# A hybrid retention and SSD layer rewritten with a lifetime-bound list scheduler, prompts first

## The chip, the cores and the metric

The kernel runs on the 8 cores of one Trainium2 chip, each core with its own part of the batch. The metric is the device time of the slowest core, in microseconds (us). A program on all eight cores has a second, slower state in some executions, in which one die, or both, has a lower granted clock. The ratios below use fast runs alone; a median is that of all runs listed, and where one of them was slow the text says so.

Engine names: PE is the matrix engine (PEld its weight loads), DVE the vector engine, ACT the activation engine, POOL the GpSimd engine, SP the engine that issues part of the DMAs. PSUM is the memory, in banks, that PE writes its products to; SBUF holds the other data on the core (one block, `arena`, in these traces). A slab is a block of weights fetched by one DMA, a ring a set of buffers used in turn. A list scheduler takes the ready operations one by one, by priority, and so fixes each engine's order before the program runs.

## The reference, cut to what matters

One layer of a backbone with two head groups. Every core gets one sample (1,024 tokens) and two prompts (256 tokens each): 1,536 tokens of width 1,024. Data lie in memory as fp32, matrix products are taken in bf16.

```python
def rms_norm(x):                      # per token and head, over 128 features
    return x * lax.rsqrt(jnp.mean(jnp.square(x), axis=-1, keepdims=True) + EPS)

def trunk_layer(x, mod, rope, s_ret0, s_ssd0, p):
    sh1, sc1, g1, sh2, sc2, g2 = jnp.split(mod, 6, axis=-1)     # from silu(cond) @ w_ada
    h = x * (1 + sc1) + sh1
    q, k, v, g, z, xbc, dt_raw = jnp.split(h @ p['w_in'], IN_SPLITS, axis=-1)
    # A: bidirectional retention, 4 heads of 128
    o_ret, sr_f, sr_b = bidir_scan(q, k, v, v, lg_f, lg_b, ...)
    o_ret = jax.nn.silu(g) * rms_norm(o_ret)                    # <- the wide rsqrt
    # B: bidirectional Mamba-2 SSD, 8 heads (conv, scan, gated norm) -> o_ssd
    mix = jnp.concatenate([o_ret, o_ssd], axis=-1) @ p['w_out']
    x = layer_norm(ALPHA * x + g1 * mix, ...)
    h2 = x * (1 + sc2) + sh2
    ffn = (jax.nn.silu(h2 @ p['w_gate']) * (h2 @ p['w_up'])) @ p['w_down']   # d_ff 2816
    return layer_norm(ALPHA * x + g2 * ffn, ...), states
```

## The kernel before

The program before records its operations, orders each engine's queue by a list scheduler with fixed buffers, and runs the stages one after the other: modulation, all projections (sample and prompts together), retention, conv and SSD, output projection, FFN. Retention works in units of one head and 512 sample tokens or 256 prompt tokens, 16 units in all. Features lie on the partitions there, so the norm's `rsqrt` is needed for a whole tile, 128 partitions by 512 or 256 columns, not for one number per token. It is taken on ACT as `exp(-0.5*ln(x))`:

```python
def rstd_from(dst, src_ps_or_sb, scale, reads, writes):
    act(dst, src_ps_or_sb, AF.Ln, ..., bias=epsb[:, 0:1], scale=scale)
    act(dst, dst, AF.Exp, writes, writes, scale=-0.5)

def ret_unit(t0, nb, h, r0, W):              # W = 512 (sample) or 256 (prompt)
    ...                                      # cut: scores, decay mask, weighted sum of v into PS(ob)
    act(sqb_[:, 0:W], PS(ob, W), AF.Square, [pk(ob)], [skey])
    mm(PS(msb, W), ones_b[:], sqb_[:, 0:W], True, True, ...)       # sum of squares over partitions
    rstd_from(rsf_[:, 0:W], PS(msb, W), 1.0 / 128.0, [pk(msb)], [rkey])
    tt(rsf_[:, 0:W], PS(ob, W), rsf_[:, 0:W], ALU.mult, ...)
    tt(oT[:, h, ...], rsf_[:, 0:W], gT[:, h, ...], ALU.mult, ..., eng=POOL)
```

Of the kernel before, what the change touches and what calls it, by code (L numbers as in the profile page):

```python
# [8 lines left out]
BF16 = mybir.dt.bfloat16  # L9
U8 = mybir.dt.uint8  # L10
AF = mybir.ActivationFunctionType
ALU = mybir.AluOpType
SZ = {F32: 4, BF16: 2}

PE, ACT, DVE, POOL, SP = "tensor", "scalar", "vector", "gpsimd", "sync"
ENGS = [PE, ACT, DVE, POOL, SP]

D = 1024
NT = 1536
NTT = 12  # L20
INC = 3592
DFF = 2816
EPS = 1e-6
ALPHA = 2.0 ** 0.25
NEG = -32768.0
SEQS = [(0, 8), (8, 2), (10, 2)]

class Op:
    __slots__ = ("idx", "eng", "fn", "is_dma", "dsem", "dval", "deps", "inc", "cval", "cost", "fin", "npend", "succ", "start", "crit", "tag", "aps")

    def __init__(self, idx, eng, fn, is_dma):
        self.idx, self.eng, self.fn, self.is_dma = idx, eng, fn, is_dma
        self.dsem, self.dval, self.deps, self.inc, self.cval = None, 0, [], False, 0
        self.cost, self.fin, self.npend, self.succ = 0.3, 0.0, 0, []
        self.start, self.crit, self.tag, self.aps = 0.0, None, '', None

class Prog:
    def __init__(self, nc):
        self.nc = nc
        self.ops = []  # L40
        self.res = {}
        self.dma_sems = {}
        self.out_dma_ops = []
        self.cur_tag = ""
        self.last_dma = {}

    @staticmethod
    def _split(key):
        if isinstance(key, tuple):
            return key[0], tuple(key[1:])  # L50
        return key, ()

    @staticmethod
    def _related(p, q):
        n = min(len(p), len(q))
        return p[:n] == q[:n]

    def _record(self, op, reads, writes):
        deps = set()
        for k in reads:  # L60
            name, p = self._split(k)
            d = self.res.setdefault(name, {})
            for q, e in d.items():
                if self._related(p, q) and e[0] is not None:
                    deps.add(e[0])
        for k in writes:
            name, p = self._split(k)
            d = self.res.setdefault(name, {})
            for q, e in d.items():
                if self._related(p, q):  # L70
                    if e[0] is not None:
                        deps.add(e[0])
                    deps.update(e[1])
        deps.discard(op)
        op.deps = sorted(deps, key=lambda o: o.idx)
        for k in reads:
            name, p = self._split(k)
            d = self.res[name]
            if p not in d:
                d[p] = [None, []]  # L80
            d[p][1].append(op)
        for k in writes:
            name, p = self._split(k)
            d = self.res[name]
            for q in [q for q in d if len(q) >= len(p) and q[:len(p)] == p]:
                del d[q]
            d[p] = [op, []]

    def op(self, eng, fn, reads=(), writes=(), cost=0.3):
        o = Op(len(self.ops), eng, fn, False)  # L90
        o.cost = cost
        o.tag = self.cur_tag
        self.ops.append(o)
        self._record(o, list(reads), list(writes))
        return o

    def dma(self, eng, fn, semkey, reads=(), writes=(), is_output=False, cost=3.0, chain=True):
        o = Op(len(self.ops), eng, fn, True)
        o.cost = cost
        o.tag = self.cur_tag  # L100
        ent = self.dma_sems.setdefault(semkey, [None, 0])
        ent[1] += 16
        o.dsem, o.dval = semkey, ent[1]
        self.ops.append(o)
        self._record(o, list(reads), list(writes))
        prev = self.last_dma.get(semkey)
        if chain and prev is not None and prev not in o.deps:
            o.deps.append(prev)
            o.deps.sort(key=lambda q: q.idx)
        self.last_dma[semkey] = o  # L110
        if is_output:
            self.out_dma_ops.append(o)
        return o

    def schedule(self):
        import heapq
        ops = self.ops
        for o in ops:
            o.succ = []
        for o in ops:  # L120
            o.npend = len(o.deps)
            for d in o.deps:
                d.succ.append(o)

        def lat(d, o):
            return 0.05 if (d.eng == PE and o.eng == PE and not d.is_dma and not o.is_dma) else 0.25

        bl = [0.0] * len(ops)
        for o in reversed(ops):
            m = 0.0  # L130
            for s_ in o.succ:
                v = bl[s_.idx] + lat(o, s_)
                if v > m:
                    m = v
            bl[o.idx] = o.cost + m
        inorder = {SP: False, POOL: False, PE: False, ACT: False, DVE: False}
# [3 lines left out]
        ready_t = {}  # L140
        nxt = {e: 0 for e in ENGS}
        eng_ops = {e: [o for o in ops if o.eng == e] for e in ENGS}
        order = {e: [] for e in ENGS}

        def push(o):
            rt = 0.0
            for d in o.deps:
                rt = max(rt, d.fin + lat(d, o))
            ready_t[o.idx] = rt
            heapq.heappush(pend[o.eng], (rt, o.idx, o))  # L150

        for o in ops:
            if o.npend == 0:
                push(o)
        done, n = 0, len(ops)
        while done < n:
            best = None
            for e in ENGS:
                if inorder[e]:
                    if nxt[e] >= len(eng_ops[e]):  # L160
                        continue
                    o = eng_ops[e][nxt[e]]
                    if o.npend != 0 or o.idx not in ready_t:
                        continue
                    st_ = max(tcur[e], ready_t[o.idx])
                    cand = (st_, o.idx, e, o)
                else:
                    p, a = pend[e], avail[e]
                    while p and p[0][0] <= tcur[e]:
                        rt, idx, o = heapq.heappop(p)  # L170
                        heapq.heappush(a, (-bl[idx], idx, o))
                    if a:
                        o = a[0][2]
                        cand = (tcur[e], o.idx, e, o)
                    elif p:
                        rt, idx, o = p[0]
                        cand = (rt, idx, e, o)
                    else:
                        continue
                if best is None or cand[:2] < best[:2]:  # L180
                    best = cand
            assert best is not None, "scheduler deadlock"
            st_, _, e, o = best
            if inorder[e]:
                nxt[e] += 1
            else:
                if avail[e] and avail[e][0][2] is o:
                    heapq.heappop(avail[e])
                else:
                    heapq.heappop(pend[e])  # L190
            o.start = st_
            o.crit = ("eng", order[e][-1]) if (order[e] and tcur[e] >= ready_t[o.idx]) else \
                ("dep", max(o.deps, key=lambda d: d.fin) if o.deps else None)
            if o.is_dma:
                tcur[e] = st_ + (1.0 if e == POOL else 0.1)
                o.fin = st_ + o.cost
            else:
                tcur[e] = st_ + o.cost
                o.fin = tcur[e]
            order[e].append(o)  # L200
            done += 1
            for s_ in o.succ:
                s_.npend -= 1
                if s_.npend == 0:
                    push(s_)
# [3 lines left out]
    def emit(self, stack, reorder=True):  # L209
        nc = self.nc  # L210
        if reorder:
            order = self.schedule()
        else:
            order = {e: [o for o in self.ops if o.eng == e] for e in ENGS}
        esem = {e: stack.enter_context(nc.semaphore("c_" + e)) for e in ENGS}
        for i, (k, ent) in enumerate(self.dma_sems.items()):
            ent[0] = stack.enter_context(nc.semaphore("d%d" % i))
        final_waits = {}
        for o in self.out_dma_ops:
            final_waits[o.dsem] = max(final_waits.get(o.dsem, 0), o.dval)  # L220

        def skip(d, o):
            return (not d.is_dma) and d.eng == PE and o.eng == PE and not o.is_dma

# [4 lines left out]
        need = {}  # L229
        for e in ENGS:  # L230
            seenpos = {}
            for o in order[e]:
                last = {}
                for d in o.deps:
                    if d.is_dma or skip(d, o):
                        continue
# [115 lines left out]
def build(debug=()):  # L352
# [35 lines left out]
    def pk(b):  # L388
        return "ps%d" % b
# [1080 lines left out]
```

## Time and profile before

| | before |
|---|---|
| median of 3 runs | 930.77 us (930.18 to 937.86) |
| profiled span | 929.3 us |
| busy PE / DVE / ACT / POOL | 767 / 388 / 346 / 282 us |
| from the start to the first dense product | about 73 us |
| projections, retention, SSD, output stage | to about 571 us |
| FFN and tail | the rest |

The profile's page of the kernel before gives busy time by engine (us, share of the span, number of instructions), and the span in 40 slices, in tenths of each slice; PEclk is the clock granted to PE, in tenths of full speed.

```profile
PE 766.9 (83%) x4299; PEld 390.4 (42%) x4376; DVE 388.2 (42%) x737; ACT 345.6 (37%) x634; POOL 282.3 (30%) x228
PE   0358899998887587766779869999999999999990
POOL 1011341011255600696220068920000000044554
PEclk9778999999999897797998979999999999999995
```

PE is at 9 tenths from about the 25th slice on: that is the FFN. Before it, PE is busy 5 to 8 tenths of many slices. The chain of waits, in order of time (start us, length us, what), says why:

```profile
4.35 45.97 DMA arena<-w_ada
50.38 9.35 DMA arena<-x
60.27 12.27 DMA arena<-w_in
...
198.67 22.78 DMA arena<-w_in
...
577.75 10.74 PE psum L437 x49
588.55 10.74 PE psum L437 x49
```

The first 73 us wait for weights and input, the last 12 of them for `w_in`; a second wait for `w_in`, of 22.78 us, comes at 199 us, and from 577 to about 845 us the chain is PE alone: 49 products per 10.74 us, 0.219 us each. Between 250 and 550 us no engine is full. The windows view of the same kernel (window, its length, busy us and number for PE, PEld, DVE, ACT, POOL, then PE clock, DMA share, GB/s) shows two stretches of it:

```profile
350.00:400.00 50.00, 37.24 (x267) 25.90 (x271) 30.75 (x56) 22.92 (x39) 18.09 (x18) 0.76 0.10 27
400.00:450.00 50.00, 34.83 (x275) 21.71 (x277) 39.81 (x54) 26.51 (x50) 34.75 (x32) 0.80 0.05 12
```

The groups of instructions by shape give what one operation costs (count, busy us, mean ns, idle time before it). For POOL:

```profile
L472 POOL TENSOR_TENSOR arena<-arena 128x1024 f32<-128x1024 f32 x46 | 107.2, 2352 | 102.0 <-ACT arena L459 83.6 <-PE psum L442 16.8 <-POOL arena L472 0.2
L472 POOL TENSOR_TENSOR arena<-arena 128x512 f32<-128x512 f32 x36 | 42.5, 1187 | 46.5 <-DVE arena L472 41.9 <-ACT arena L459 4.0 <-DVE arena L479 0.5
```

A product or sum of 512 columns takes POOL 1.19 us, one of 1,024 columns 2.35 us: 2.3 ns per column. The trace names them TENSOR_TENSOR; by the program, all of them are products, sums and the like.

### The profile page before, as it was taken

The page shows a single profiled execution, that of the slowest core. Times are in us where ns is not written, and L with a number is a line of the kernel's source. Part 1 is how long each engine was busy: PE and PEld are TensorE (multiplying, and loading weights), DVE is VectorE, ACT ScalarE, POOL GpSimd, SP SyncE. Part 2 cuts the span into 40 slices and gives each one's busy share as a digit, 9 for nine tenths or more (in the row PEclk, how much of TensorE's full clock was granted, in tenths as well). Part 3 has the DMA queues.
Part 4 walks back from the last instruction along what each step waited for, and adds up shares of the span by engine and source line. Part 5 has one row for each costly group of instructions (what it writes and reads, how often), then busy time and mean ns, then how long its engine had stood idle before and what let it go on. Part 6 is the DMA issues. An engine that isn't in the chain of part 4 may idle for free.

```text
span 929.3 us, 13094 instructions; the slowest of 8 cores (915.7 to 929.3 us)
## 1 busy us (share of the span) xinstructions
PE 766.9 (83%) x4299; PEld 390.4 (42%) x4376; DVE 388.2 (42%) x737; ACT 345.6 (37%) x634; POOL 282.3 (30%) x228
## 2 busy tenths in 40 slices
PE   0358899998887587766779869999999999999990
PEld 0343334444432246444545444444444444544440
DVE  0143772011488415668877772112111122333224
ACT  0256215221266664454533964111111121243333
POOL 1011341011255600696220068920000000044554
PEclk9778999999999897797998979999999999999995
DMA  9979234599680200200005440395433332311111
GB/s 202 201 146 145 46 47 68 72 147 158 93 113 1 57 1 1 57 2 23 2 1 196 139 74 1 46 143 72 57 46 46 46 46 33 82 45 46 46 65 72
DMA packets 61282, 67.02 MB, mean 72 GB/s; under 512 B 5920, under 2 KB 52384, under 8 KB 60960
## 3 DMA queue, kind: packets, MB, share of 16 engines
q0 software_dynamic: 48064, 40.98, 31.3%
q1 hardware_dynamic: 13152, 25.20, 8.2%
q8 instruction: 37, 0.61, 0.2%
q14 instruction: 29, 0.24, 0.1%
HBM read 98.76 MB, written 8.39 MB: 115 GB/s over the span
## 4 chain that ended last, share of the span: by engine, by line
PE 57%; DMA 12%; issue 10%; DVE 9%; POOL 5%; ACT 5%; DVEq 0%; another core or an unknown queue 0%; ACTq 0%; POOLq 0%; SPq 0%
PE psum L437 56%; DVE arena L472 7%; DMA arena<-w_ada 5%; POOL arena L472 5%; ACT arena L459 5%; DMA arena<-w_in 4%; PE psum L442 2%; DVE arena L488 1%; DMA arena<-sret 1%; DMA arena<-x 1%; DMA y<-arena 1%; ACT L459 0%; POOL arena L505 0%; DVE arena L494 0%; DVE arena L479 0%
## 5 line engine op out<-in xcount | busy, mean ns | idle before, releaser
L437 PE MATMUL psum<-arena 128*128 128x512 bf16 (+8 forms) x4047 | 732.4, 332 | 123.3 <-ACT arena L459 41.9
L437 PEld LDWEIGHTS psum<-arena 128*128 128x128 bf16 (+2 forms) x4124 | 356.4, 104 | 492.1 <-issue 194.1
L472 POOL TENSOR_TENSOR arena<-arena 128x1024 f32<-128x1024 f32 (+4 forms) x152 | 226.1, 1506 | 257.5 <-ACT arena L459 107.1
L459 ACT ACTIVATE arena<-psum 128x512 bf16<-128x512 f32 (+3 forms) x212 | 123.3, 615 | 355.1 <-PE psum L437 322.6
L459 ACT ACTIVATE arena<-arena 128x512 bf16<-128x512 f32 (+8 forms) x255 | 166.7, 684 | 164.4 <-DVE arena L488 100.8
L472 DVE TENSOR_TENSOR arena<-psum,arena 128x512 f32<-128x512 f32 (+5 forms) x205 | 126.2, 642 | 119.9 <-PE psum L437 83.7
L472 DVE TENSOR_TENSOR arena<-arena,psum 128x512 bf16<-128x512 bf16 (+2 forms) x112 | 79.4, 740 | 190.8 <-PE psum L437 107.9
L472 DVE TENSOR_TENSOR arena<-arena 128x1 f32<-128x1 f32 (+9 forms) x99 | 56.5, 579 | 24.7 <-ACT arena L459 19.9
L442 PE MATMUL psum<-arena 128*128 128x128 f32 (+1 forms) x252 | 47.4, 334 | 16.2 <-ACT arena L459 8.2
L488 DVE SCALAR_TENSOR_TENSOR arena<-arena 128x512 f32<-128x512 f32 (+1 forms) x84 | 50.5, 629 | 12.4 <-ACT arena L459 11.6
L505 POOL DMA_DIRECT2D arena<-w_gate x11 | 9.8, 892 | 144.0 <-PE psum L437 126.4
L459 ACT ACTIVATE arena<-psum,arena 128x128 bf16<-128x128 f32 (+4 forms) x92 | 42.8, 544 | 26.0 <-PE psum L437 20.4
L494 DVE CAST arena<-psum 128x512 bf16<-128x512 f32 (+2 forms) x37 | 22.7, 631 | 69.1 <-PE psum L437 66.4
L442 PEld LDWEIGHTS psum<-arena 128*128 128x128 f32 (+1 forms) x252 | 38.0, 172 | 23.5 <-issue 20.5
L479 DVE TENSOR_SCALAR arena<-arena 128x128 f32<-128x128 f32 (+6 forms) x90 | 24.1, 291 | 33.9 <-PE psum L437 16.7
L505 POOL DMA_DIRECT2D arena<-w_ada x12 | 10.8, 905 | 81.0 <-PE psum L437 80.1
L459 ACT ACT_TABLE_LOAD x15 | 19.2, 1283 | 29.6 <-DMA arena<-rows 22.1
L505 POOL DMA_DIRECT2D arena<-w_down x6 | 4.6, 766 | 83.2 <-PE psum L437 83.2
L494 DVE COPY arena<-psum 128x512 f32<-128x512 f32 (+2 forms) x27 | 17.2, 647 | 27.4 <-PE psum L437 22.1
L505 POOL DMA_DIRECT2D arena<-w_in x7 | 6.2, 898 | 64.9 <-DMA arena<-x 54.5
L482 DVE TENSOR_SCALAR arena<-arena 128x1 f32<-128x1 f32 (+3 forms) x38 | 10.9, 315 | 19.3 <-ACT arena L459 19.1
L482 DVE TENSOR_SCALAR arena<-psum,arena 128x512 bf16<-128x512 f32 x12 | 9.3, 804 | 7.9 <-PE psum L442 7.9
(20 smaller groups left out, 44.6 us busy)
## 6 DMA issues: line engine op xcount, KB each, us to landing
arena<-w_ada POOLq DMA_DIRECT2D x12, 1024.0 KB, 13.8
arena<-x SPq DMA_DIRECT2D x3, 2048.0 KB, 12.4
arena<-w_in POOLq DMA_DIRECT2D x6, 1024.0 KB, 16.4
arena<-x SPq DMA_DIRECT2D x12, 512.0 KB, 4.3
arena<-w_gate POOLq DMA_DIRECT2D x11, 512.0 KB, 5.8
arena<-w_up POOLq DMA_DIRECT2D x11, 512.0 KB, 8.4
y<-arena SPq DMA_DIRECT2D x11, 512.0 KB, 2.6
arena<-w_down POOLq DMA_DIRECT2D x5, 1024.0 KB, 14.2
```

The lines of the kernel that those rows point to most:

```text
L437: o_ = P.op(PE, lambda e: e.matmul(out, lhsT=lhsT, rhs=rhs, start=start, stop=stop), reads, writes, cost=c)
L442: o_ = P.op(PE, lambda e: e.transpose(out=out, in_=in_, identity=ident_f[:]), list(reads) + ["const"], writes, cost=0.1)
L459: o_ = P.op(ACT, lambda e: e.activation(out=out, in_=in_, func=func, **kw), reads, writes, cost=c)
L472: o_ = P.op(eng, lambda e: e.tensor_tensor(out=out, in0=in0, in1=in1, op=op), reads, writes, cost=vcost(eng, fs(out), f))
L479: o_ = P.op(eng, lambda e: e.tensor_scalar(out=out, in0=in0, scalar1=s1, scalar2=None, op0=op0), reads, writes, cost=c)
L482: o_ = P.op(eng, lambda e: e.tensor_scalar(out=out, in0=in0, scalar1=s1, scalar2=s2, op0=op0, op1=op1), reads, writes, cost=c)
L488: o_ = P.op(DVE, lambda e: e.scalar_tensor_tensor(out=out, in0=in0, scalar=scalar, in1=in1, op0=op0, op1=op1), reads, writes, cost=vcost(D ...
L494: o_ = P.op(eng, lambda e: e.tensor_copy(out=out, in_=in_), reads, writes, cost=vcost(eng, fs(out), 1.0))
L505: o_ = P.dma(eng, lambda e: e.dma_start(out=out, in_=in_), key, reads, writes, is_output, cost=2.0 + nb / 150e3, chain=chain)
```

## The change

The intent is overlap. The program is new: a scheduler in which an operation may choose between engines, PSUM banks are given out by pool and lifetime, and SBUF buffers are placed by lifetime instead of by hand. Prompts go first, then the sample; SSD and retention (now in chunks of 512 tokens) run beside the projections; weights are packed by the host into contiguous slabs of 128 x 4,096. Among many smaller edits, the wide `rsqrt` moves from two ACT operations to one POOL operation, a `pow` with exponent -0.5, which spares ACT two operations. The `rsqrt` of the other norms, one number per token, becomes a `pow` on POOL too: 36 operations of one column. The diff has 2,805 lines; this is part, with cuts marked.

```diff
-    def rstd_from(dst, src_ps_or_sb, scale, reads, writes):
-        act(dst, src_ps_or_sb, AF.Ln, list(reads) + ["epsb"], writes, bias=epsb[:, 0:1], scale=scale)
-        act(dst, dst, AF.Exp, writes, writes, scale=-0.5)
 ... (cut)
+    def vcost(eng, out, ins, kind):              # what the new scheduler believes
+        n = fsize(out)
+        if eng == POOL:
+            return 0.12 + n * 0.0022
 ... (cut)
+    rstS, rS1, rS0 = Ring("stS", 1, 512), Ring("S1", 2, 256, BF16), Ring("S0", 2, 256)
+
+    def ret_unit(h, ck, o0, nt, W, qT, kT, v3, gT, cross):
 ... (cut: scores, mask, weighted sum into the PSUM bank o)
+        sq = rsq()
+        act(sq[:, 0:W], o, AF.Square)
+        m = P.ps("mix", W)
+        mm(m, ones_b, sq[:, 0:W], True, True)
+        ms = rms()
+        affine(ms[:, 0:W], m, c32[:, 0:1], eps4[:, 0:1])
+        rg = rrg()
+        tt(rg[:, 0:W], ms[:, 0:W], mhalf[:, 0:1].to_broadcast([128, W]), ALU.pow, POOL)
+        tt(rg[:, 0:W], rg[:, 0:W], gT[:, o0:o0 + W], ALU.mult, POOL)
+        o1 = o0 % 512
+        tt(oR[ck][:, h, o1:o1 + W], o, rg[:, 0:W], ALU.mult)
 ... (cut)
+    ffn("all", LV_DENSE, [[hb[4]], [hb[4]], [oB]])
```

(`mhalf` holds -0.5.)

## The prediction

> **What bounds the kernel now.** The busy table gives PE 767 of 929 us, DVE 388, ACT 346, POOL 282, but the stretches split in two. From about 571 us (FFN) PE is saturated: the chain of waits shows 49 matmuls per 10.74 us, 0.219 us each, at granted clock 1.00, up to the tail: 1,584 matmuls of 512 columns. Before that, PE takes almost twice its need: 53 us with no weights (the chain is a w_ada DMA from 4 to 50 us at DMA share 1.00), then projections with two DMA waits (12 us and 23 us on w_in), then from 250 to 550 us retention and SSD in sequence, where PE is busy 35 to 42 of each 50 us at clock 0.76 to 0.95 and no engine is full: handoffs.
>
> **Work removed, added, moved.** Counted from the built programs; start-to-start durations from the trace (512 columns 0.2155 us warm, 256: 0.109, 128 bf16: 0.056, 128 fp32: 0.112, 2 columns: 0.025). The Trainium skill, "TensorE: Matmul & The Clock Gate" (Wait - 56ns, not 53.3ns?), states N/2.4 GHz plus 2.5 ns warm and N/1.2 GHz cold; the trace agrees (216 and 427 ns).
> - 512-column matmuls 2,808 to 2,600 (bf16 mask matmuls gone, chunked retention, gate rows as 2-row products): minus 45 us.
> - Fewer fp32 transposes; 128-column bf16 matmuls rise by about 480 (v per head, k transposes): plus 22 us net. w_ada column products 384 to 256: minus 3.
> - PE need: about 697 to 669 us. So the gain must come from overlap, not from less work.
> - DVE: by trace means (0.685 us per 512-column PSUM operand, 0.756 for the two-input SBUF form, 0.2-0.3 for tiny ones) about 430 us, of which some 325 before the FFN, against PE's 322 there. POOL about 290 us plus 16 wide `pow`s, whose cost no trace shows. ACT about 220.
> - Weights are packed on the host: 8 KB packets in place of 512 B to 2 KB. Before, bf16 packets took 98 ns per 1,024 B and 173 ns per 2,048 B; estimate by that slope 0.61 us per 8 KB, some 25% more rate. In the first 50 us [...]the start is limited elsewhere; I expect only a few us there.
>
> **On the critical path.** Start to dense PE work: 55 us. Projections, conv and both SSDs: PE need 155, I expect 175. Prompt heads 42, expect 50. Sample heads plus prompt out stage 96, expect 110 (per sample head PE 19.6 us and DVE about 20 us: balanced). Sample out stage 35, expect 45. FFN 343. Tail 12 (before about 22). Sum 790 us.
>
> **Prediction: 790 us, 80% range 750 to 840.** Chances: faster 0.95, same 0.03, slower 0.02.
>
> **What would show it.** FFN again 0.216-0.219 us per matmul, starting near 435 us instead of 571. PE busy total about 690 to 720, above 88% of the span. DVE above 80% in the sample-head stretch, clock above 0.95 between 60 and 430 us. First dense matmul at 50-60 us.
>
> **What would make it wrong.** POOL `pow` of 512 columns at 10 us or more would make POOL the limit in the sample heads (plus 40 to 100 us). POOL also issues the weight DMAs, which wait for late matmuls; blocked there it starves DVE. The static order rests on modelled costs; if real ones differ, in-order engines stall each other. Low side: if DVE overlaps nearly perfectly, 745.

## The result, and the profile after

| | before | after |
|---|---|---|
| median | 931.51 us (4 runs) | 1783.91 us (4 runs, one of them slow at 1830.5) |
| ratio after / before | | 1.9125 (95%: 1.9051 to 1.9199) |
| busy PE / DVE / ACT / POOL | 767 / 388 / 346 / 282 | 724 / 404 / 265 / 1286 us |
| matmul and transpose records of PE in the trace (weight loads) | 4,299 (4,376) | 4,432 (4,432) |

Some matmul records can be missing from a trace; the weight loads are the better count. A ratio here is the mean time of one kernel's fast runs over that of the other's of the same rounds, so it is not quite the ratio of the medians. The change nearly doubles the time. The page of the kernel after, the same rows as above:

```profile
PE 724.2 (41%) x4432; PEld 377.4 (21%) x4432; DVE 403.5 (23%) x821; ACT 265.4 (15%) x435; POOL 1286.3 (72%) x370
PE   1999840102030280003200130003020797999997
POOL 5025789897969749997999989997999391000185
PEclk9999975556565595556655575556565998999998
```

PE, DVE and ACT do about the work that was predicted. POOL is busy 1,004 us longer than before, and from the 7th to the 31st slice PE is busy for 0 to 3 tenths, but for one slice, while POOL is nearly full. The groups by shape for POOL; one operation of 128x256 as the timeline lists it, and the group of the one-column `pow`s; and the chain of waits in order of time:

```profile
L655 POOL TENSOR_TENSOR arena<-arena 128x512 f32<-128x512 f32 x95 | 764.6, 8065 | 25.0 <-ACT arena L632 13.5 <-DVE arena L655 5.7 <-DVE arena L689 4.3
L655 POOL TENSOR_TENSOR arena<-arena 128x256 f32<-128x256 f32 x16 | 334.2, 20906 | 3.1 <-ACT arena L632 3.1
```

```profile
329.28 41.15 POOL L655 TENSOR_TENSOR arena<-arena 128x256 f32<-128x256 f32 x1 [1.25 <-ACT arena L632]
L655 POOL TENSOR_TENSOR arena<-arena 128x1 f32<-128x1 f32 x36 | 22.6, 628 | 86.2 <-DVE arena L661 83.3 <-DVE arena L655 1.2 <-DVE arena L669 0.9
```

```profile
235.91 40.97 issue
276.94 41.03 issue
...
665.53 82.17 POOL arena L655
748.94 83.17 POOL arena L655 x2
...
1476.30 10.10 DMA arena<-w_gu
1486.53 282.80 PE psum L607 x1296
```

Two readings to learn here. First, a mean can hide two kinds of work in one group: the 95 operations of 128x512 have a mean of 8.1 us, but no single one takes that. Listed one by one, eight of them take 81.9 to 82.2 us each, and the other 87 about 1.2 us ((764.6 - 8 x 82.0) / 87 = 1.25). Of the 16 of 128x256, eight take 41.1 us and eight about 0.7 us. There are just eight sample units and eight prompt units of retention: the long ones are the `pow`s, 985 us in all. The 36 `pow`s of one column take 0.63 us each: the cost grows with the columns. Second, the page's summary of the chain puts 32% on POOL and 27% on "issue", time in which the engine waited for nothing that the profile shows. The 41 us pieces called "issue" start and end with the prompt `pow`s (the list of POOL's operations has one from 235.6 to 276.9 and the next from 276.9 to 318.0): a profile that cannot name a wait is not a profile without one.

The waits view (who waits <- for whom: us in total, times, longest us) and the windows of the kernel after:

```profile
DVE arena L655 <- POOL arena L655: 817.4, 16, 83.2
PE psum L607 <- POOL arena L655: 730.4, 8, 161.5
```

```profile
200.00:250.00 50.00, 36.84 (x371) 21.64 (x371) 31.91 (x56) 15.89 (x33) 33.09 (x26) 0.86 0.90 149
250.00:300.00 50.00, 0.00 (x0) 0.00 (x0) 0.00 (x0) 0.00 (x0) 50.00 (x2) 0.50 0.10 21
700.00:800.00 100.00, 0.00 (x0) 0.00 (x0) 2.76 (x4) 0.00 (x0) 99.86 (x3) 0.50 0.00 0
```

DVE waits for POOL sixteen times, PE behind it for up to 161 us. In 250 to 300 us only POOL works, and in 700 to 800 us only POOL and, for 2.8 us, DVE. PE's granted clock is 0.50 meanwhile, while PE has nothing to do; in the first experiment below, with the same order and without that idle time, PE's clock is 0.95 on average, so it is not a cause of its own. The FFN, with the same 1,584 products, is again PE alone.

### The profile page after: what moved, and what is told of

Same layout as the page of the kernel before. It is cut to its first block, busy times and chain, and to the rows that moved or that the text cites. A ratio compares the mean times of both kernels' runs of the same rounds, so it can differ in the third digit from the quotient of the medians.

```text
span 1781.5 us, 13396 instructions; the slowest of 8 cores (1772.7 to 1781.5 us)
## 1 busy us (share of the span) xinstructions
PE 724.2 (41%) x4432; PEld 377.4 (21%) x4432; DVE 403.5 (23%) x821; ACT 265.4 (15%) x435; POOL 1286.3 (72%) x370
## 4 chain that ended last, share of the span: by engine, by line
PE 34%; POOL 32%; issue 27%; DMA 3%; DVE 3%; ACT 1%; SPq 0%; DVEq 0%; POOLq 0%; ACTq 0%
PE psum L607 32%; POOL arena L655 32%; DMA arena<-x 2%; DVE arena L655 1%; PE psum L610 1%; DVE arena L669 1%; ACT arena L632 1%; DMA arena<-w_gu 1%; DMA arena<-w_ada 1%; DVE arena L689 0%; SPq L182 0%; DVE psum L1174 0%; DVEq L501 0%; DVE arena L661 0%; POOL arena L661 0%
## 5 line engine op out<-in xcount | busy, mean ns | idle before, releaser
L655 POOL TENSOR_TENSOR arena<-arena 128x512 f32<-128x512 f32 (+5 forms) x218 | 1230.0, 5662 | 184.9 <-DVE arena L661 83.3
L607 PE MATMUL psum<-arena 128*128 128x512 bf16 (+7 forms) x4228 | 698.9, 325 | 1030.7 <-POOL arena L655 730.4
L607 PEld LDWEIGHTS psum<-arena 128*128 128x128 bf16 (+1 forms) x4228 | 352.4, 102 | 1372.6 <-issue 1088.6
L655 DVE TENSOR_TENSOR arena<-psum,arena 128x512 f32<-128x512 f32 (+4 forms) x208 | 128.8, 635 | 1056.6 <-POOL arena L655 813.3
L632 ACT ACTIVATE arena<-psum 128x512 bf16<-128x512 f32 (+2 forms) x201 | 113.5, 573 | 969.5 <-PE psum L607 955.7
L632 ACT ACTIVATE arena<-arena 128x512 bf16<-128x512 f32 (+6 forms) x106 | 79.4, 765 | 491.1 <-DVE arena L669 378.4
L669 DVE SCALAR_TENSOR_TENSOR arena<-arena 128x1 f32<-128x1 f32 (+2 forms) x108 | 63.4, 597 | 17.5 <-POOL arena L655 10.9
L632 ACT ACTIVATE arena<-psum,arena 128x512 bf16<-128x512 f32 (+3 forms) x72 | 47.2, 674 | 34.3 <-PE psum L610 21.6
L610 PE MATMUL psum<-arena 128*128 128x128 f32 (+1 forms) x204 | 29.3, 296 | 14.5 <-DMA arena<-x 7.8
L661 POOL TENSOR_SCALAR arena<-arena 128x128 bf16<-128x128 f32 (+2 forms) x43 | 23.7, 560 | 13.8 <-ACT arena L632 10.5
L655 DVE TENSOR_TENSOR arena<-arena 128x1 f32<-128x1 f32 (+9 forms) x75 | 31.4, 425 | 6.7 <-ACT arena L632 2.9
L632 ACT ACT_TABLE_LOAD x20 | 25.7, 1283 | 16.1 <-PE psum L607 11.0
```

The source lines that it names most:

```text
L607: return P.add({PE: (c, lambda e: e.matmul(R(out), lhsT=R(lhsT), rhs=R(rhs), start=start, stop=stop))}, [lhsT, rhs], [out])
L610: return P.add({PE: (0.12, lambda e: e.transpose(out=R(out), in_=R(in_), identity=R(ident_f)))}, [in_, ident_f], [out])
L632: fn = lambda e: e.activation(out=R(out), in_=R(in_), func=func, **{k: R(v) for k, v in kw.items()})
L655: fn = lambda e: e.tensor_tensor(out=R(out), in0=R(in0), in1=R(in1), op=op)
L661: fn = lambda e: e.tensor_scalar(out=R(out), in0=R(in0), scalar1=R(s1), scalar2=None, op0=op0)
L669: fn = lambda e: e.scalar_tensor_tensor(out=R(out), in0=R(in0), scalar=R(scalar), in1=R(in1), op0=op0, op1=op1, **{k: R(v) for k, v in kw. ...
```

## The experiments

The main theory (A): POOL's `pow` is slow by itself, about 160 ns per column, and the kernel stands still for nearly all of it. The rivals: (B) the broadcast second operand makes the operation slow, not `pow`; (C) the new order, its buffers or the host's packing are at fault; (D) the order rests on a false cost, and a scheduler that knew the cost would hide the `pow`. All runs gave the reference's result unless said otherwise. Every run stands beside runs of the kernel before on the same chip.

### Another operation in the same place

The same program, order, operands and buffers, with a product in place of the power. The result is wrong (relative error 1.44).

```diff
-        tt(rg[:, 0:W], ms[:, 0:W], mhalf[:, 0:1].to_broadcast([128, W]), ALU.pow, POOL)
+        tt(rg[:, 0:W], ms[:, 0:W], mhalf[:, 0:1].to_broadcast([128, W]), ALU.mult, POOL)
```

> The 16 wide pow instructions on POOL become multiplies with the same operands (same shapes, same broadcast second operand); the order of every engine is unchanged and the result is wrong on purpose. Theory A (the pow itself runs at about 160 ns per column on POOL: 8 of 82 us and 8 of 41 us, 984 us in all, and nothing else is wrong): each falls to about 1.2 us, POOL busy from 1286 to about 320 us, the span to 790 us (760 to 830), the granted clock above 0.93. Rival B (the stride-0 second operand is what is slow on POOL, not pow): the multiplies stay near 80 and 40 us and the span near 1780. Rival C (the static order or the tight memory of the new program is itself slow, pow hides it): the multiplies fall but the span stays above 900.

Measured: 827.13 us (825.96 to 829.15), ratio 0.8861 (0.8814 to 0.8907). POOL's groups and the page of this run:

```profile
PE 704.3 (85%) x4360; PEld 371.0 (45%) x4432; DVE 406.2 (49%) x821; ACT 265.2 (32%) x435; POOL 317.1 (38%) x370
L655 POOL TENSOR_TENSOR arena<-arena 128x512 f32<-128x512 f32 x95 | 117.9, 1258 | 25.0 <-ACT arena L632 13.5 <-DVE arena L655 5.7 <-DVE arena L689 4.3
L655 POOL TENSOR_TENSOR arena<-arena 128x256 f32<-128x256 f32 x16 | 10.4, 675 | 3.2 <-ACT arena L632 3.1
```

One word of the source is worth 1783.91 - 827.13 = 957 us, and POOL's busy time falls by 969 us. B falls in the form that a broadcast operand is slow whatever the operation, for it stayed. (A wide `pow` with a full second operand was not tried; the one-column `pow`s have no broadcast, and their 0.63 us fits the same line, 0.47 us plus 0.159 us per column.) C falls as the cause of the loss, for order and buffers stayed. It also shows how little of the cost was hidden: 957 of 969 us.

The traces of both agree up to the first `pow`: the 1,600th weight load starts at 231 us in the kernel after and at 230 us here, the 1,700th at 324 and 244 us, the 2,000th at 626 and 317 us.

### Is it the exponent?

The `pow` stays, its exponent becomes 1.0 (wrong, a single run).

```diff
+    one1 = P.buf("one1", 1)
+    memset(one1, 1.0)
 ...
-        tt(rg[:, 0:W], ms[:, 0:W], mhalf[:, 0:1].to_broadcast([128, W]), ALU.pow, POOL)
+        tt(rg[:, 0:W], ms[:, 0:W], one1[:, 0:1].to_broadcast([128, W]), ALU.pow, POOL)
```

> The changed kernel with the wide pow's exponent 1.0 in place of -0.5 (wrong result on purpose), same order. If the cost lies in the operation whatever the values, 82 us per 512 columns again and a span within 1 per cent of 1784; if it depends on the exponent, much less.

Measured: 1794.12 us. POOL's groups:

```profile
L655 POOL TENSOR_TENSOR arena<-arena 128x512 f32<-128x512 f32 x95 | 765.2, 8072 | 26.6 <-ACT arena L632 14.6 <-DVE arena L655 5.8 <-DVE arena L689 4.3
L655 POOL TENSOR_TENSOR arena<-arena 128x256 f32<-128x256 f32 x16 | 334.3, 20907 | 3.1 <-ACT arena L632 3.0
```

The durations are those of exponent -0.5 to a thousandth, and the 16 long operations again sum to 985 us. These two exponents cost the same; others were not tried.

### The other way round: `pow` in the kernel before

The old program, with only its wide `rsqrt` exchanged (the line that fills `mhalf` with -0.5 is cut).

```diff
-        rstd_from(rsf_[:, 0:W], PS(msb, W), 1.0 / 128.0, [pk(msb)], [rkey])
+        ts(rsf_[:, 0:W], PS(msb, W), 1.0 / 128.0, ALU.mult, [pk(msb)], [rkey], s2=EPS, op1=ALU.add)
+        tt(rsf_[:, 0:W], rsf_[:, 0:W], mhalf[:, 0:1].to_broadcast([128, W]), ALU.pow, [rkey, "mhalf"], [rkey], eng=POOL)
```

> The kernel before, with one thing of the change put into it alone: in its 16 retention units the Ln and Exp on ACT become one scaling pass on DVE and a pow on POOL (8 of 512 columns, 8 of 256); result must be right. Theory A (the pow costs about 160 ns per column wherever it stands): POOL busy from 282 to about 1260 us, the span from 930 to 1750 to 1900 us, as the retention stage has little to run beside it. Rival C (it is slow only in the new program, by its order or its tight memory): within 5 per cent of 930.

Measured: 1902.23 us (1898.98 to 1905.48), ratio 2.0444 (2.0371 to 2.0517). POOL's groups:

```profile
L472 POOL TENSOR_TENSOR arena<-arena 128x512 f32<-128x512 f32 x44 | 698.3, 15878 | 46.8 <-DVE arena L472 41.4 <-ACT arena L459 4.2 <-DVE arena L482 0.7
L472 POOL TENSOR_TENSOR arena<-arena 128x256 f32<-128x256 f32 x8 | 329.1, 41136 | 1.1 <-DVE arena L482 0.9
```

Here the 128x256 group holds the eight prompt `pow`s alone, so its mean is the duration itself: 41.1 us. The old program, with another scheduler, other buffers and other weights in memory, loses 1902.23 - 930.86 = 971 us, as much as the new one. The cost belongs to the operation.

### Telling the scheduler

`pow` stays, and the scheduler gets its measured cost. With the longer lifetimes that follow, the buffers no longer fitted (217,600 of 212,800 bytes per partition), until one FFN slab was loaded later; that is the second edit.

```diff
-            return 0.12 + n * 0.0022
+            return 0.47 + n * 0.159 if kind == ALU.pow and n > 1 else 0.12 + n * 0.0022
 ... (cut: `tt` passes its operation on to vcost)
-    ffn("all", LV_DENSE, [[hb[4]], [hb[4]], [oB]])
+    ffn("all", LV_DENSE, [[hb[4]], [oB], [oB]])
```

> The pow stays on POOL, but the scheduler is told what it costs (0.47 us + 0.159 us per column), and so makes an order for it (one FFN weight slab is fetched later, because the stretched lifetimes did not fit in memory). Theory A: POOL still has some 1286 us of work, so the span stays at 1550 to 1750 us. Rival D (the harm is mainly the order made from a wrong cost, in-order engines held up behind pow): the span falls below 1400.

Measured: 1720.48 us, ratio 1.8426 (1.8279 to 1.8574). The page of this run:

```profile
PE 727.0 (42%) x4363; PEld 377.9 (22%) x4432; DVE 407.6 (24%) x822; ACT 269.5 (16%) x439; POOL 1283.9 (75%) x367
```

D falls: knowing the cost gains 63 us of 957. POOL alone still has 1,284 us of work, so no order that leaves the `pow`s there could come down to the 931 us of the kernel before. In the 16 stretches of the `pow`s, PE is busy for 106 us of their 985 here and for 39 us in the kernel after (sums of the windows view over these stretches): the order did change, and this scheduler found little to put beside them. The false cost is a fault of the program, but a small one beside the operation.

### The old `rsqrt` in the new program

Two forms, both correct. In the first, `pow` becomes Ln and Exp on ACT, in the second Ln reads PSUM directly, as it did before, and the separate scale-and-add goes.

```diff
-        tt(rg[:, 0:W], ms[:, 0:W], mhalf[:, 0:1].to_broadcast([128, W]), ALU.pow, POOL)
+        act(rg[:, 0:W], ms[:, 0:W], AF.Ln)
+        act(rg[:, 0:W], rg[:, 0:W], AF.Exp, scale=-0.5)
```

> Each wide pow is replaced by Ln and Exp on ACT, as the kernel before did it; result must be right. The scheduler makes a new order. Theory A: span 800 us (770 to 850); ACT busy rises from 265 by about 20 us plus table loads (20 now, perhaps 35 to 45, at 1.28 us each). Rival C: above 900.

```diff
-        ms = rms()
-        affine(ms[:, 0:W], m, c32[:, 0:1], eps4[:, 0:1])
-        tt(rg[:, 0:W], ms[:, 0:W], mhalf[:, 0:1].to_broadcast([128, W]), ALU.pow, POOL)
+        act(rg[:, 0:W], m, AF.Ln, bias=eps4[:, 0:1], scale=1.0 / 32.0)
+        act(rg[:, 0:W], rg[:, 0:W], AF.Exp, scale=-0.5)
```

> As e2, but Ln reads PSUM directly with scale 1/32 and the bias, so the separate scaling pass is gone (16 instructions fewer on ACT or DVE). Theory A: 0 to 10 us below e2; right result. If ACT table loads are what limits, equal to e2.

Measured: 835.94 us, ratio 0.895 (0.8891 to 0.9009), and 834.93 us (833.45 to 836.51), ratio 0.8942 (0.8896 to 0.8989). The two are the same within their intervals. So the correct new program without wide `pow` is 10.6% faster than the kernel before: the rest of the change does what it was meant to do. Over the program with the one-microsecond stand-in of the first experiment that is 834.93 - 827.13 = 8 us; the order of operations differs between the two, so not all of it need be Ln and Exp. ACT does 37 table loads of 1.283 us in the second form, against 20 in the kernel after: 17 x 1.283 = 22 us more of ACT's time, while the whole program is only 8 us longer. (The Trainium skill, "ScalarE: Activation LUTs", What ACT_TABLE_LOAD costs, gives about 1283 ns for such a load; all traces here agree. It adds a drain of about 1380 ns per switch, which no run here shows apart.)

It is still 45 us over the 790 us predicted. The chain, the waits from 225 to 300 us and a window of the second form say where:

```profile
239.59 31.66 DMA oret<-arena
530.49 10.49 DMA arena<-w_gu
```

```profile
PE psum L607 <- DMA oret<-arena: 9.9, 1, 9.9
```

```profile
250.00:300.00 50.00, 26.95 (x177) 13.44 (x178) 8.23 (x23) 15.70 (x27) 4.76 (x8) 0.69 0.82 153
```

The store of a prompt state takes 31.66 us from issue to landing. The ring `stS` has one buffer, so the next head's state waits until this store has landed. PE works on during a part of that time; idle for the store it is once, for 9.9 us. The store shares the DMA engines with the weights that stream in at the same time (DMA share 0.82 in this window). A second wait stands in the FFN: 10.5 us for its fourth slab of `w_gu`, whose issue sits in POOL's queue behind 24 products and sums on the residual (the kernel after has it too: the piece of 10.10 us in its chain).

### Four state buffers; FFN loads first; both

Three runs on top of the second form above.

```diff
-    rstS, rS1, rS0 = Ring("stS", 1, 512), Ring("S1", 2, 256, BF16), Ring("S0", 2, 256)
+    rstS, rS1, rS0 = Ring("stS", 4, 512), Ring("S1", 2, 256, BF16), Ring("S0", 2, 256)
```

> e2b with four buffers in place of one for the prompt retention states on their way to memory. In e2b the chain of waits holds one store for 31.7 us (239.6 to 271.2 us), queued behind weight loads, while the next head's copy needs its buffer. Theory E (that buffer is what stalls the prompt heads): the wait goes and the span falls by 10 to 30 us. Rival F (the weight loads themselves are late, the DMA engines being 89 per cent busy from 237 to 318 us; the store only stands in the same queue): the span falls by less than 8 us and waits on w_in or w_ada take its place.

```diff
         for sl in range(11):
             P.level = LV_BG
             af = first_after[sl] if sl < len(first_after) else [fmm[sl - len(first_after)]]
+            P.level = 0
             w = slab_load("gu%d" % sl, w_gu_d[sl], 4096, after=af)[0]...
```

> e2b with the FFN weight loads given first priority in the scheduler: in e2b POOL issues the fourth slab at 530.5 us, behind 24 products and sums over x1 (56 us of POOL), and PE waits 11 us for it. Theory: the wait on w_gu near 530 us goes, the span falls by 8 to 15 us. Rival: POOL's x1 work then delays something else (the residual of the last norms) and nothing is gained.

> e5 and e6 together. If the two stalls are independent, the gains add: 810 to 820 us, 15 to 30 us below e2b. Result must be right.

Measured: 817.74 us, ratio 0.8793 (0.877 to 0.8815), with the ring of four; 820.52 us, ratio 0.8812 (0.8784 to 0.8841), with the loads first (six runs, one of them slow at 879.34; the five fast ones have a median of 818.94); 804.47 us (803.04 to 806.42), ratio 0.8647 (0.8626 to 0.8669), with both, a little below the 810 us expected at best. By the medians of fast runs the gains are 17, 16 and 30 us. These runs were on another chip than the second form; by the ratios the gains are 14, 12 and 27 us, each uncertain by some 4 to 5 us because of the interval of the second form. Within that they add, as waits in different stages should.

With four buffers the next head's store goes out at 253 instead of 273 us, yet the first store stays in the chain. From the run with both edits, the chain and a window:

```profile
237.26 30.30 DMA oret<-arena
250.00:300.00 50.00, 35.18 (x228) 18.08 (x229) 16.50 (x37) 17.15 (x31) 6.69 (x11) 0.75 1.00 184
```

PE is idle for this store for only 2.7 us now, and for 5.9 us for `w_in`. So the length of a piece of the chain, which runs from issue to landing, is not what its removal is worth; and the crowded DMA engines, the rival named in the expectation, remain: they are full from 250 to 300 us, and PE is busy for 35 of these 50 us.

### Taking two loads out of the crowded stretch

On top of both edits, the last two slabs of `w_ada` (the gate that only the last stage needs) are loaded after the sample's output stage, not between the prompt heads.

```diff
-        else:
-            ada_load(8 + h, [last_h[h - 1]])
-            gate_row(1, h - 2)
 ...
+    for half in range(2):
+        ada_load(10 + half, [oB])
+        gate_row(1, half)
```

> e7 with the two w_ada slabs and the row product of the second gate, which only the last norms need, moved from the prompt heads to after the sample heads. In e7 the DMA engines are 96 per cent busy from 230 to 300 us and PE is busy 50 of 70 us there. Theory F (the weight loads of that stretch are the limit): 4 MB read less there, the span falls 6 to 14 us below e7's 804, and the sample heads begin earlier. Rival: handoffs between engines are the limit there, no gain beyond 3 us. Result must be right.

Measured: 796.67 us (794.8 to 800.09), ratio 0.8548 (0.8516 to 0.858), on another chip than the run with both edits. The ratios' intervals lie apart, so it is a gain, of some 1%. The profiled spans differ by 3 us only (799.1 and 802.0), but the run profiled here was the slowest of five and the one before the fastest of four; the medians differ by 8. The 1,900th weight load starts at 277 us in place of 286. After it, 16 weight loads of the gate have moved, to 467 to 472 us; the 2,720th of this run starts at 412 us, its counterpart in the run with both edits (the 2,736th) at 420. So 8 us are gained where the loads were taken away. Their 16 products of 512 columns now stand in the FFN, where PE is full: by an estimate of 16 x 0.216 us, 3.5 us are given back there. This is the fastest version, correct, and 14.5% below the kernel before. Its page and two of its windows:

```profile
PE 702.2 (88%) x4361; PEld 371.3 (46%) x4432; DVE 404.0 (51%) x818; ACT 290.9 (36%) x466; POOL 308.9 (39%) x359
300.00:350.00 50.00, 44.35 (x318) 25.45 (x321) 42.10 (x84) 24.10 (x36) 24.90 (x26) 0.98 0.22 59
350.00:400.00 50.00, 48.08 (x340) 26.45 (x345) 41.25 (x66) 23.26 (x32) 26.39 (x24) 0.98 0.49 96
```

In the kernel before, PE was busy 36 and 37 of these 50 us.

### What packing is worth

On top of both edits, `w_ada` is read from its original layout, in rows of 2 KB, instead of from packed slabs.

```diff
-    w_ada_d = di("w_ada", [12, 128, 4096])
+    w_ada_d = di("w_ada", [1024, 6144])
 ...
-        ada[s] = slab_load("ada%d" % s, w_ada_d[s], 4096)
+        ada[s] = slab_load("ada%d" % s, ada_src(s), 4096)
```

> e7 with one part of the change undone: w_ada is read from its original layout (rows of 2 KB, 1 KB packets after the cast) in place of packed slabs. Same order and waits on all engines. By packet times (98 ns per 1,024 B before, 625 ns per 8,192 B after: 25 per cent more time per byte) the first four slabs cost the start 6 to 8 us more if the packets set the pace there, and the later slabs something between 200 and 300 us: 6 to 15 us above e7. If the start is limited elsewhere (my prediction), less than 4 us there.

Measured: 811.46 us (six runs, one of them slow at 921.38), ratio 0.8706 (0.8678 to 0.8735). Against the packed version, which ran on another chip, that is 7 us by the medians and 5.5 us by the ratios (0.0059 of 931 us). Its chain at the start:

```profile
3.22 24.08 DMA arena<-w_ada
...
27.84 24.77 DMA arena<-w_in
```

The first weight load of PE starts at 20 us in place of 15, and the 1,300th at 206 us where the packed versions have 198 to 203. So most of it is lost in the start. Packing the twelve slabs of `w_ada` is worth a few us, the size that was predicted, and no more; the packing of the other weights was not undone. That the start is "limited elsewhere", as the prediction has it, does not hold as it stands: some 5 us of the start do follow the packets.

### Tried and left open

A wide `pow` on DVE was refused by the compiler in two forms (`tensor_scalar` and `tensor_tensor`), so what it would cost there is not known. The value of the overlap alone, of SSD and retention beside the projections, was not measured; no run undoes it. That the new program without wide `pow` gains 97 us is shown; how it splits between overlap, chunked retention and fewer products is not.

## Why the prediction was wrong, point by point

The prediction was 790 us with a range of 750 to 840; measured were 1783.91. Its direction was wrong, too.

**The step that failed: the cost of the 16 wide `pow`s.** The prediction lists "POOL about 290 us plus 16 wide `pow`s, whose cost no trace shows", and its sum of stages then holds nothing for them. Under the dangers it puts "512 columns at 10 us or more" and "plus 40 to 100 us". Measured: 82 us for 512 columns, 41 us for 256, 985 us in all; the exchange for a product took 957 us off the whole. The danger was named and mis-sized by a factor of ten or more. (The rest of the POOL term was right: without the wide `pow`s POOL is busy for 1286 - 985 = 301 us.) The trace's figure for POOL's other operations was 2.3 ns per column; the one thing that was not in the trace took 160, seventy times as much. A term that cannot be sized from a trace or a page does not belong in a sum at zero with a chance of 0.02 for "slower". The Trainium skill, "GPSIMD Engine Reference", Elementwise — side-by-side cycle accounting, measures about 2.6 cycles per element for a two-input operation, with `add` as its example; from its 1.2 GHz one estimates 1.1 us for 512 columns, and products (1.19 us) come close. `pow` takes the same instruction name in the trace and costs 65 to 70 times as much at this width. The page does not speak of it, and the figure must not be carried over.

**"Would make POOL the limit in the sample heads".** Too narrow. It stopped the prompt heads first (eight `pow`s, from 235 to 611 us), then the sample heads. And POOL was not merely the limit, as an engine with much to do beside the others is: 99% of what it cost was on the critical path (957 of 969 us), and in its 985 us PE was busy for 39 us, DVE for 24 and ACT for 10, because each unit's product waits for its `pow` with a PSUM bank taken, and the queues of the in-order engines have the next units behind it. That last link is argued from the program and the waits; with the cost told, the scheduler found a place beside them for only 67 us more of PE work (106 less 39).

**"The static order rests on modelled costs; if real ones differ, in-order engines stall each other".** The model did differ, 1.25 us against 82. But correcting it gained 63 us only, with this scheduler. This was the smaller part.

**The rest of the sum, with the `pow` gone.** The correct form with Ln and Exp took 834.93 us, inside the range. By stages, from its profiled run of 835.4 us:

| stage ends at | predicted | Ln/Exp form | fastest version |
|---|---|---|---|
| conv and SSD done (1,600th weight load) | 230 us | 232 us | 232 us |
| FFN begins (first of the last 1,584 weight loads; of the last 1,600 in the fastest version, where 16 of the gate moved into the FFN) | 435 us | 463 us | 437 us |
| from there to the last product | 343 us | 360 us | 351 us |
| tail | 12 us | 11.6 us | 11.4 us |

So start, projections and SSD together, and the tail, were right to 2 us. The first is partly luck: the first dense product came at 50 us and not at 55, and the stages after it took 182 us and not 175. From there to the FFN 205 us were predicted and 231 taken, 26 too few, and the FFN was 17 us short (2 + 26 + 17 = 45). The terms that were too small were those for the prompt heads, for which "42, expect 50" took PE's need and left the DMA out (a single store buffer behind the weights), and for the FFN, which left out the wait for a slab behind POOL's work. With four buffers the FFN begins at 449 us, 14 us earlier; with the loads first it takes 345 us. Undoing both gave 27 to 30 of the 45 us. Which of the prompt heads, sample heads and output stages the other 12 us before the FFN belong to was not separated.

**The signs that were named.** PE busy 690 to 720: 714 in the Ln/Exp form, right; 724 in the kernel after, where the clock fell to 0.50 in the idle stretches. PE above 88% of the span: 85%, and 88% in the fastest version only (71 of its 4,432 product records are missing, so it may be a little more). DVE above 80% in the sample heads: 82 to 84% in the fastest version. First dense product at 50 to 60 us: at 48 to 51 us with packed weights. A clock above 0.95 from 60 to 430 us: wrong from 200 to 350 us even without `pow` (0.69 in the window shown, where PE is busy for 27 of 50 us and waits for DMA). FFN products at 0.216 to 0.219 us: right. Fewer us of ACT, about 220: it was 265. DVE about 430: it was 404.

## What to carry to other kernels

Before an operation is moved to an engine, look for that very operation on that engine in a trace, at that width; if there is none, measure one before you build on it, and do not price it by its neighbours, even when the profile gives both the same instruction name. A group's mean that fits none of its members is the first place to look when an engine's busy time jumps, and the quickest test is to exchange the one operation for a cheap one in the same place and order, even at the price of a wrong result. When a scheduler spreads work over all engines, look next at what each queue issues besides computing: a store with one buffer and a load behind 24 products cost some 30 us here.

## What the Trainium skill lacked or had wrong

- "GPSIMD Engine Reference", Elementwise — side-by-side cycle accounting: no figure for `pow`, and no warning that operations of one instruction can differ this much. Measured on POOL, fp32, 128 partitions: product of 512 columns 1.19 us, `pow` of 512 columns 82 us, of 256 columns 41 us, of one column 0.63 us, so 160 ns per column (82 - 41.1 over 256), the same for exponents -0.5 and 1.0. Its key point that DVE is about twice as fast for elementwise work says nothing of this.
- "ScalarE: Activation LUTs", What it computes, advises a reciprocal followed by a square root for `rsqrt`. That section does not name Ln and Exp for it, which gave a correct result here, with 8 us more for the whole kernel than a stand-in product on POOL, 17 more table loads included.
- "TensorE: Matmul & The Clock Gate", Part 1, tells the reader to budget 13/16 of the clock once three cores of a die run dense products. In the FFN all eight cores do, and the granted clock of all eight was 1.00 (before: 600 to 800 us; fastest version: 550 to 750 us), with 49 products of 512 columns in 10.74 us (0.219 us each; at 13/16 it would be an estimated 0.27). The measurement decides: no such limit showed in the fast runs. It may be what a slow run is: in the slow one of the run with `w_ada` unpacked, the four cores of one die had mean clocks of 0.812 to 0.818, near 13/16, and the other four 0.953 to 0.968; no trace of it was kept. The same page's 56 ns and 216 ns for 128 and 512 columns agree with the trace.
